# Decay rows of a chunked SSD: stored to memory once and read back by broadcast transfers, in place of 128 selection products on TensorE

## The chip, the cores and the metric

The kernel runs on one core of one Trainium2 chip. The metric is device microseconds of one execution of the whole program; the kernel before takes 1842.9 us, the median of 3 runs (1841.74 to 1843.09). A difference under 0.2% (3.7 us) is about what a measurement of this kernel cannot tell from no change.

## The reference, cut to what matters

One decoder layer on a sequence of 1024 tokens and 1024 channels: an SSD (Mamba-2) mixer and a differential-attention mixer side by side, merged by gates, then a gated conv-FFN. The change lies in the SSD, which works in chunks of 128 tokens, 16 heads in 2 groups of 8. Of one chunk and one head:

```python
a_cum = jnp.cumsum(la, axis=2)
seg = a_cum[:, :, :, None] - a_cum[:, :, None, :]
decay = jnp.exp(jnp.where(causal, seg, -jnp.inf))
cb = jnp.einsum('bclgn,bcsgn->bclsg', cc, bc)
y_diag = jnp.einsum('bclsgr,bcsgrp->bclgrp', cb[..., None] * decay, xd)
```

So for every chunk and head a 128x128 matrix exp(a_cum[l] - a_cum[s]) is wanted, for s up to l, with the running sum of one token set against that of another.

## The kernel before, in words

**Layout.** The kernel holds tokens or channels on the 128 partitions. Wide products are done as three products of float32r halves (high x high, high x low, low x high). `SL` is a ring of 43 slots of 128x1024 float32 in SBUF that tiles take and give back. SyncE (SP) issues nearly all transfers, in the order of the program; a transfer that has to wait holds up all those behind it. At most eight transfers are outstanding, since each waits for the one eight places ahead. PE, DVE, ACT and SP run in an order written out by hand (`tc.manual_schedule`); the order of GpSimd (POOL) and of what lies between those blocks is decided when the program is built.

**Ahead of the SSD.** While the z projection runs (`thirds`, 24 groups of 24 products), `decays_a` and `decays_b` compute dt, the running sum `acum` (128 tokens on the partitions; 8 chunks x 16 heads along the row) and its exponentials. `decays_b` also splits `acum` into a float32r high part and a rest, side by side in `acx` (L866 to L869). `decays_c` (L871 to L877) clears `acT`, turns `acx` chunk by chunk with 8 transposes, and copies the turned rows: `acT` then holds, for each token along the row, the 16 high parts and the 16 rests on 32 partitions.

**The SSD loop.** There are 16 units `u`, one for each chunk and group (`c, g = divmod(u, 2)`). Step `u` of the loop prepares unit `u + 1` and finishes unit `u`. In program order a step does the following.

- `chunk_in(u + 1)`: 4 transposes of x, the product of B and C, a transpose of B, into the PSUM tile `px`; ACT copies them out (L1077, L1078), DVE makes `cbm` and `xd` (L1079, L1080), POOL makes `xdd` and the skip term of `y` (L1082, L1083).
- `chunk_decay(u + 1)`: 8 selection products (L1092), one for each head. The weights are a column of `sel` widened to 128, so that each product adds the head's high part and rest and puts the row a_cum[l] on all 128 partitions of the PSUM tile `pb`. ACT then makes relu(acum[s] - pb) out of PSUM into the decay tile `M[g]` (L1096, 8 instructions) and exp of its negative in place (L1098, 2 instructions).
- `chunk_mask(u + 1, 0)`, and later `(u + 1, 1)`: DVE multiplies half of the decay tile by `cbm` (L1103).
- `chunk_out(u)`: the product with the carried state (`po`, L1110), 8 products with the decay tile as weights (`py`, L1114, each in two passes of 64 columns), and sums on DVE and POOL (L1111, L1116, L1119, L1120).
- `chunk_state(u)`: the product for the next state (`pst`, L1128), and after every second unit `chunk_norm`.

Between these, `fill` puts in products of the v projection (L1028 to L1030, 128x512), `sum_dn` puts in sums of weights for a later stage (L790 to L797 on DVE, with loads `wdr` and stores `wtd`), and `run_bg` puts in small pieces. `M` are two tiles, one for each group. `px` and `pb` take turns in two PSUM buffers (`ps_mm`). SP issues in each step stores of v (`vd`), loads and stores of the weight sums (`wdr`, `wtd`), and by turns the loads of x (`xch`) and z (`zt`) and the store of y (`yd`).

Of the kernel before, what the change touches and what calls it, by code (L numbers as in the profile page):

```python
# [62 lines left out]
def kernel(ctx: ExitStack, tc: tile.TileContext, a: dict, out: bass.AP, dbg=None):  # L63
    nc = tc.nc
    V, A, G, T, SP = nc.vector, nc.scalar, nc.gpsimd, nc.tensor, nc.sync
# [15 lines left out]
    def ps_mm(name):  # L81
        return pmm.tile([P, 2, HALF], F32, tag="mm", name=name, bufs=2)

    def ps_wa(name):
        return pp.tile([P, HALF], F32, tag="wa", name=name, bufs=2)
# [44 lines left out]
    ident = const("ident", [P, P])  # L130
# [279 lines left out]
    SP.dma_start(tri, a["tri"])  # L410
    maskneg = const("maskneg", [P, P])
    SP.dma_start(maskneg, a["maskneg"])
    selr = const("selr", [P, NH])
    SP.dma_start(selr, a["sel"])
    sel = const("sel_r", [P, NH], F32R)

    zd = [dp.tile([P, D], F32, tag=f"zd{i}", name=f"zd{i}") for i in range(8)]
    vd = [dp.tile([P, D], F32, tag=f"vd{i}", name=f"vd{i}") for i in range(8)]
# [180 lines left out]
    part = lambda t, k: t[k // 2][:, k % 2, :]  # L599

    with tc.manual_schedule(engines={EN.PE, EN.DVE, EN.Activation, EN.SP}):
        V.tensor_copy(sel, selr)
        vev = SL.get("vev", F32, (P, 2, HALF))
        cgv = [None, [SL.get(f"xc{n}1") for n in "gv"]]
        for n in ("t2", "t1", "t3"):
# [200 lines left out]

    sm1 = SL.get("sm1", F32, (P, 8, 8, NH))
    sm2 = SL.get("sm2", F32, (P, 1024))
    hi_t = SL.get("hi_t", F32R, (P, 8, NH))
    dtr, dt, la, acum, ea, cd, dte, sp0_ = (sm1[:, n] for n in range(8))  # L810
    acx = sm2[:, 0:256].rearrange("p (c h) -> p c h", c=8)
    sp1_ = sm2[:, 256:384]
    cbm = sm2[:, 384:640].rearrange("p (g l) -> p g l", g=2)
    btok = sm2[:, 640:896].rearrange("p (g l) -> p g l", g=2)
    ev = [SL.get(f"ev{i}", F32, (P, 2, HALF)) for i in range(2)]
    n_ev = 0

    acT = SL.get("acT", F32R, (P, S))
    aexp = const("aexp", [P, NH])

    CH = 8 * NH
    f = lambda t: t.rearrange("p c h -> p (c h)")
# [34 lines left out]
    def decays_b():  # L857
        pa = ps_wa("acum_ps")
        T.matmul(pa[:, :CH], tri, f(la), start=True, stop=True)
        T.matmul(pa[:, CH : 2 * CH], ones, f(la), start=True, stop=True)  # L860
        V.tensor_copy(f(acum), pa[:, :CH])
        A.activation(f(ea), f(acum), AF.Exp)
        A.activation(f(cd), pa[:, CH : 2 * CH], AF.Exp)
        V.tensor_tensor(f(dte), pa[:, CH : 2 * CH], f(acum), op=ALU.subtract)
        A.activation(f(dte), f(dte), AF.Exp)
        hi_r = hi_t  # L866
        V.tensor_copy(hi_r, acum)
        V.tensor_copy(acx[:, :, :NH], hi_r.bitcast(F32))
        V.tensor_tensor(acx[:, :, NH:], acum, hi_r.bitcast(F32), op=ALU.subtract)  # L869

    def decays_c():  # L871
        V.memset(acT.bitcast(F32), 0.0)
        for half in range(2):
            pt = ps_wa(f"acT_ps{half}")
            for q in range(4):
                T.transpose(pt[:32, q * P : (q + 1) * P], acx[:, 4 * half + q, :], ident)
            V.tensor_copy(acT[:32, half * HALF : (half + 1) * HALF], pt[:32, :])  # L877

    dec = None
    adas = [SL.get(f"adas{i}") for i in range(4)]  # L880
# [18 lines left out]
    with tc.manual_schedule(engines={EN.PE, EN.DVE, EN.Activation, EN.SP}):  # L899
        for t_, (c0, wdt) in enumerate(thirds):  # L900
# [4 lines left out]
            for i in range(8):  # L905
                nz = 8 * t_ + i
                ps = (ps_x((1, 3, 2, 0)[nz % 4], f"z{c0}_{i}") if nz < 22 else ps_wa(f"z{c0}_{i}"))[:, :wdt]
                half, q = divmod(i, 4)
# [39 lines left out]
                if nz == 17:  # L948
                    xch = [SL.get(f"xch{i}", F32, (P, KD, P)) for i in range(2)]
# [7 lines left out]
    BT, CT = [xbcT[8], xbcT[9]], [xbcT[10], xbcT[11]]  # L957
    vev = SL.get("vev", F32, (P, 2, HALF))

    SL.put(hi_t)  # L960


    GW = HALF
# [2 lines left out]
    xd = SL.get("xd")  # L966
    xdd = SL.get("xdd")
    xtk = SL.get("xtk")
    M = [SL.get(f"M{g}", F32, (P, RH, P)) for g in range(2)]
    prev = [SL.get(f"prev{i}", F32, (P, 2, GW)) for i in range(2)]  # L970
    tt = SL.get("tt")
    zt = SL.get("zt")
# [89 lines left out]
    def load_z(c):  # L1062
        SP.dma_start(zt, zd[c])
# [21 lines left out]

    def chunk_decay(u):
        c, g, tok, hs, gs, y = at_(u)
        pm = ps_mm(f"pb{c}_{g}")
        for b4 in range(2):
            for r in range(4):  # L1090
                h = g * RH + 4 * b4 + r
                T.matmul(pm[:, b4, r * P : (r + 1) * P], sel[:, h : h + 1].broadcast_to([P, P]), acT[:, tok], start=True, stop=True)  # L1092
        for b4 in range(2):
            for r in range(4):
                h = g * RH + 4 * b4 + r
                A.activation(M[g][:, 4 * b4 + r, :], pm[:, b4, r * P : (r + 1) * P], AF.Relu, scale=-1.0, bias=acum[:, c, h : h + 1])  # L1096
            mv = M[g][:, 4 * b4 : 4 * b4 + 4, :]
            A.activation(mv, mv, AF.Exp, scale=-1.0)  # L1098

    def chunk_mask(u, b4):  # L1100
        c, g, tok, hs, gs, y = at_(u)
        mv = M[g][:, 4 * b4 : 4 * b4 + 4, :]
        V.tensor_tensor(mv, mv, cbm[:, g : g + 1, :].broadcast_to([P, 4, P]), op=ALU.mult)  # L1103

    def chunk_out(u, mask):
        c, g, tok, hs, gs, y = at_(u)
        po = prev[(c + 1) % 2]
        if c > 0:
            pq = ps_wc(f"po{c}_{g}")
            T.matmul(pq, CT[g][:, tok], po[:, g, :], start=True, stop=True)  # L1110
            V.tensor_tensor(v3(tt[:, gs]), v3(pq), bc64(ea[:, c, hs]), op=ALU.mult)  # L1111
        py = ps_wb(f"py{c}_{g}")
        for r in range(RH):
            T.matmul(py[:, r * 64 : (r + 1) * 64], M[g][:, r, :], xd[:, g * GW + r * 64 : g * GW + (r + 1) * 64], start=True, stop=True)  # L1114
        mask()
        V.tensor_tensor(y[:, gs], py, y[:, gs], op=ALU.add)  # L1116
        if c > 0:
            if c < 7:
                G.tensor_tensor(v3(prev[c % 2][:, g, :]), v3(po[:, g, :]), bc64(cd[:, c, hs]), op=ALU.mult)  # L1119
            G.tensor_tensor(y[:, gs], y[:, gs], tt[:, gs], op=ALU.add)  # L1120
# [48 lines left out]
    def fetch_seq(n):  # L1169
        if n < len(seq):  # L1170
            kind, b = seq[n]
            seq_w[n] = wp.tile([P, KD, P], F32, tag="wraw", name=f"{kind}{b}_raw", bufs=3)
            SP.dma_start(seq_w[n].rearrange("p k c -> p (k c)"), a[kind][b])

    load_z(0)
    wdr = [[SL.get(f"wdr{i}{j}", F32, (P, 2, HALF)) for j in range(2)] for i in range(2)]
    wds = [SL.get(f"wds{i}", F32, (P, 2, HALF)) for i in range(2)]
# [8 lines left out]
    with tc.manual_schedule(engines={EN.PE, EN.DVE, EN.Activation, EN.SP}):  # L1186
        for k in range(2):
            down_load(k)
        chunk_in(0)
        fill(2)  # L1190
        chunk_decay(0)
        chunk_mask(0, 0)
        chunk_mask(0, 1)
        lamt = const("lamt", [P, 2, 64])
        lams = const("lams", [P, 2])
        nlam = const("nlam", [P, 1])
        rl = rows[:, R_LAM : R_LAM + 256].rearrange("p (a b d) -> p a b d", a=2, b=2)
        V.tensor_tensor(lamt, rl[:, :, 0, :], rl[:, :, 1, :], op=ALU.mult)
        V.reduce_sum(lams, lamt, axis=AX.X)
        A.activation(lams, lams, AF.Exp)  # L1200
        V.tensor_tensor(nlam, lams[:, 1:2], lams[:, 0:1], op=ALU.subtract)
        V.tensor_scalar(nlam, nlam, -LAM_INIT, None, op0=ALU.add)
        subw = const("subw", [P, 1])
        V.tensor_scalar(subw, vec[:, V_SUB : V_SUB + 1], 1.0 - LAM_INIT, None, op0=ALU.mult)
        fill(4)
        for u in range(16):
            nxt = u + 1 < 16
            if nxt:
                chunk_in(u + 1)
            fill(2)  # L1210
            run_bg(2)
            sum_dn(u, 0)
            if nxt:
                chunk_decay(u + 1)
            run_bg(1)
            sum_dn(u, 1)
            if nxt:
                chunk_mask(u + 1, 0)
            fill(2)
            chunk_out(u, (lambda: chunk_mask(u + 1, 1)) if nxt else (lambda: None))  # L1220
            fill(3)
            run_bg(3)
            sum_dn(u, 2)
            chunk_state(u)
            fill(1 if u % 3 else 0)
            run_bg(1)
            sum_dn(u, 3)
            if u % 2 == 1:
                chunk_norm(u // 2)
            if u == 11:  # L1230
                assert next(sums_dn, None) is None
                SL.put(*wdr[0], *wdr[1], *wds)
                yr = [SL.get(f"yr{i}") for i in range(4)]
                ropc, rops = SL.get("ropc"), SL.get("rops")
                SP.dma_start(ropc, a["ropc"])
                SP.dma_start(rops, a["rops"])
                fetch_seq(0)
                fetch_seq(1)
            elif u == 12:
                load_y(0)  # L1240
        fill(16 * KD)
        run_bg(len(bg))
    SL.put(*yt, xd, xdd, xtk, *M, *prev, tt, zt, acT, sm1, sm2, *xch, *BT, *CT)

# [1113 lines left out]
def host_arrays(i):  # L2358
# [41 lines left out]
        "ident": np.eye(128, dtype=np.float32),  # L2400
        "tri": (s[:, None] <= s[None, :]).astype(np.float32),
        "maskneg": np.where(s[None, :] <= s[:, None], np.float32(0), np.float32(NEG)).astype(np.float32),
        "sel": ((np.arange(128)[:, None] % 16 == np.arange(16)[None, :]) & (np.arange(128)[:, None] < 32)).astype(np.float32),
        "ropc": ropc,
        "rops": rops,
    }
# [14 lines left out]
```

## Time and profile before

| | |
|---|---|
| median of 3 runs | 1842.9 us (1841.74 to 1843.09) |
| span of the profiled execution | 5463.1 us; no time of that execution beside the span is given |
| busy in that span | PE 5447.4, DVE 1312.2, ACT 898.9, POOL 139.0 us |
| moved by transfers | 326.22 MB, mean 60 GB/s over the span |
| SSD loop in that span | from about 1140 to 1740 us |

The profiled execution lasted three times as long as the timed ones. In it the products of TensorE follow one another without a pause, and each takes much longer than a third of the timed run would allow, though the granted clock is shown as full; the other engines are busy for a quarter of the span or less. So its durations on DVE, ACT, POOL and the transfers can be read as they stand, while those on PE have to be scaled, and a wait for PE is longer in it than in a timed run. A row of the views reads: line, engine, operation, tiles out<-in, shapes, count, then busy microseconds and mean nanoseconds of one, then idle time of the engine just before, with what ended it. The chain of waits lists start, length and line of the work that ended last.

### The profile page before, as it was taken

Reading aid. Unit: us, or ns where it says so; the run is one execution under the profiler, and the core shown is the slowest. Engines: PE = TensorE matmul, PEld = TensorE weight load, DVE = VectorE, ACT = ScalarE, POOL = GpSimd, SP = SyncE. Lnnn points to the kernel's source line nnn. Section 1 sums busy time; section 2 is a strip of 40 time slices with the busy share of each in tenths; the row PEclk is TensorE's granted clock in tenths of the full one; section 3 lists DMA queues with packets and bytes.
Section 4 is the critical chain, followed back from the end, with each engine's and each line's share of the span. In section 5 each row is a group of like instructions: output and inputs, shape, how many; then the busy total and the mean of one; then the engine's idle time right before and its main releaser. Section 6 shows DMA issues by size and latency. Waiting matters only on the chain.

```text
span 5463.1 us, 24362 instructions
## 1 busy us (share of the span) xinstructions
PE 5447.4 (100%) x8922; PEld 3303.6 (60%) x8922; DVE 1312.2 (24%) x1984; ACT 898.9 (16%) x1744; POOL 139.0 (3%) x128
## 2 busy tenths in 40 slices
PE   9999999999999999999999999999999999999999
PEld 4555557766665555566677776556555555555555
DVE  4122222222221200022222231212333333332211
ACT  3111110011111100011122221102212111121210
POOL 0000000001110000000000000000000000000000
DMA  4021012212111212121122112210011111123221
GB/s 165 31 77 46 29 35 72 70 64 100 64 67 46 54 35 81 35 52 47 48 72 69 56 47 95 81 46 31 31 44 39 44 35 41 40 71 116 87 63 60
DMA packets 131368, 326.22 MB, mean 60 GB/s; under 512 B 14881, under 2 KB 39089, under 8 KB 131250
## 3 DMA queue, kind: packets, MB, share of 16 engines
q1 hardware_dynamic: 130290, 321.53, 18.2%
q0 software_dynamic: 960, 3.15, 0.2%
q8 instruction: 70, 1.15, 0.1%
q14 instruction: 48, 0.39, 0.0%
HBM read 229.45 MB, written 95.17 MB: 59 GB/s over the span
## 4 chain that ended last, share of the span: by engine, by line
PE 100%; issue 0%; ACT 0%; POOL 0%; DVE 0%; DMA 0%; DVEq 0%; POOLq 0%; ACTq 0%
PE upx L1822 4%; PE upx L1823 4%; PE upx L1821 4%; PE o L1515 4%; PE v L1028 2%; PE z L116 2%; PE v L1029 2%; PE z L118 2%; PE z L117 2%; PE xx L534 2%; PE so L117 2%; PE so L118 2%; PE xx L532 2%; PE upy L1821 2%; PE upy L1822 2%; PE upy L1823 2%
## 5 line engine op out<-in xcount | busy, mean ns | idle before, releaser
L1515 PEld LDWEIGHTS o<-vt,aT 128*128 128x128 f32 x576 | 201.1, 415 | 39.5 <-issue 33.8
L1821 PE MATMUL upx<-t,wu_t 128*128 128x512 f32 x264 | 218.9, 829 | 0.0
L1823 PE MATMUL upx<-t,wu_t 128*128 128x512 f32 x264 | 218.7, 828 | 0.0
L1822 PE MATMUL upx<-t,wu_t 128*128 128x512 f32 x264 | 218.7, 828 | 0.0
L1515 PE MATMUL o<-vt,aT 128*128 128x128 f32 x576 | 214.2, 578 | 0.0
L1456 PE MATMUL sc<-kst,qst 128*128 128x512 f32 (+2 forms) x192 | 141.7, 742 | 0.0
L1457 PE MATMUL sc<-klo,qst 128*128 128x512 f32 (+2 forms) x192 | 141.4, 746 | 0.0
L118 PE MATMUL so<-yT,w_ssd_o_lo 128*128 128x512 f32 x128 | 140.8, 1100 | 0.0
L117 PE MATMUL so<-yT,w_ssd_o_hi 128*128 128x512 f32 x128 | 140.8, 1100 | 0.0
L116 PE MATMUL so<-yT,w_ssd_o_hi 128*128 128x512 f32 x128 | 139.3, 1088 | 0.0
L1503 ACT COPY aT<-at 128x512 f32<-128x512 f32 (+2 forms) x96 | 45.9, 479 | 562.2 <-PE at L1502 562.2
L1822 PEld LDWEIGHTS upx<-t,wu_t 128*128 128x128 f32 x264 | 93.5, 354 | 63.8 <-issue 63.8
L1821 PEld LDWEIGHTS upx<-t,wu_t 128*128 128x128 f32 x264 | 93.4, 354 | 63.7 <-issue 62.7
L1823 PEld LDWEIGHTS upx<-t,wu_t 128*128 128x128 f32 x264 | 92.3, 350 | 63.8 <-issue 63.8
L1114 PEld LDWEIGHTS py<-xd,M 128*128 128x128 f32 x256 | 107.1, 596 | 34.8 <-issue 34.8
L1028 PE MATMUL v<-wv_hi,hT 128*128 128x512 f32 x96 | 121.5, 1266 | 0.0
L116 PE MATMUL z<-wz_hi,hT 128*128 128x346 f32 (+1 forms) x144 | 121.1, 841 | 0.0
L118 PE MATMUL z<-wz_hi,hT 128*128 128x346 f32 (+1 forms) x144 | 119.7, 832 | 0.0
L117 PE MATMUL z<-wz_lo,hT 128*128 128x346 f32 (+1 forms) x144 | 119.1, 827 | 0.0
L1502 PE MATMUL at<-ident,p 128*128 128x128 f32 x288 | 117.1, 576 | 0.0
L2184 PE MATMUL dx<-wdt_hi,g_hi 128*128 128x512 f32 x132 | 109.5, 830 | 0.0
L2186 PE MATMUL dx<-wdt_hi,g_lo 128*128 128x512 f32 x132 | 109.2, 827 | 0.0
(553 smaller groups left out, 10212.8 us busy)
## 6 DMA issues: line engine op xcount, KB each, us to landing
adas<-in_w_ada SPq DMA_DIRECT2D x32, 512.0 KB, 3.9
wdr<-in_w_down SPq DMA_DIRECT2D x22, 512.0 KB, 5.5
wtd<-wds SPq DMA_DIRECT2D x22, 512.0 KB, 2.9
wuf<-in_w_up SPq DMA_DIRECT2D x22, 512.0 KB, 3.5
gld_s<-gsum SPq DMA_DIRECT2D x22, 512.0 KB, 2.6
gst<-gld_s SPq DMA_DIRECT2D x20, 512.0 KB, 4.3
wdt_raw<-wtd SPq DMA_DIRECT2D x20, 512.0 KB, 3.9
wuv<-in_w_up SPq DMA_DIRECT2D x19, 512.0 KB, 3.6
```

What stands on the lines that cost most here:

```text
L116: T.matmul(ps, lh, rh, start=(i == 0), stop=False)
L117: T.matmul(ps, lh, rl, start=False, stop=False)
L118: T.matmul(ps, ll, rh, start=False, stop=(i == n - 1))
L1028: T.matmul(ps, xh_, wh, start=(k == 0), stop=False)
L1456: T.matmul(sc[:, n0:n1], qs_[s][:, tsl], ks_[s][:, n0:n1], start=True, stop=False)
L1457: T.matmul(sc[:, n0:n1], qs_[s][:, tsl], kl[s][:, n0:n1], start=False, stop=True)
L1502: T.transpose(ptr[:, k * P : (k + 1) * P], pt_[i % 2][0][:, (k0 + k) * P : (k0 + k + 1) * P], ident)
L1515: T.matmul(po_of[j, grp][:, qi, :], at[:, k, :], vt[j % 2][:, kt, :], start=(kt == 0), stop=(kt == i))
L1821: T.matmul(out_, wh, xh_, start=(k == 0 and first), stop=False, skip_group_check=not first)
L1822: T.matmul(out_, wh, xl_, start=False, stop=False, skip_group_check=not first)
L1823: T.matmul(out_, wl, xh_, start=False, stop=(k == end), skip_group_check=not first)
L2184: T.matmul(o, gh[:, kk, tsl], wh, start=(k == 0 and not more), stop=False, skip_group_check=more)
```

## The change

The 128 selection products, the split of `acum`, `acT`, `sel` and its load go. `decays_c` now turns `acum` once (128 tokens x 128 chunk-head pairs), copies the result out of PSUM and stores it to memory as `acd`, 16 rows of 1024, one for each unit: 8 heads x 128 tokens. `load_decay(u)` reads row `u` into a decay tile with the row repeated on all 128 partitions (a transfer of 512 KB on the SP queue). ACT's relu then works in place in that tile, reading SBUF where it read PSUM. There are three decay tiles in place of two, used in turn. The first three are loaded ahead of the loop; the load for unit `u + 2` stands at the start of step `u`, from step 1 on, ahead of `chunk_in(u + 1)`; its tile is that of unit `u - 1`, so that it waits for the products `py` of that unit. In the built program POOL also does the skip term (L1083) in another place among its instructions, and a subtraction (L637) that stood behind the copy of `sel` on DVE at the start of the program stands earlier.

```diff
-    selr = const("selr", [P, NH])
-    SP.dma_start(selr, a["sel"])
-    sel = const("sel_r", [P, NH], F32R)
...
-        V.tensor_copy(sel, selr)
...
-    hi_t = SL.get("hi_t", F32R, (P, 8, NH))
-    acx = sm2[:, 0:256].rearrange("p (c h) -> p c h", c=8)
+    acr = sm2[:, 0:128]
-    acT = SL.get("acT", F32R, (P, S))
+    acd = dp.tile([2 * 8, D], F32, tag="acd", name="acd")
...
-        hi_r = hi_t
-        V.tensor_copy(hi_r, acum)
-        V.tensor_copy(acx[:, :, :NH], hi_r.bitcast(F32))
-        V.tensor_tensor(acx[:, :, NH:], acum, hi_r.bitcast(F32), op=ALU.subtract)
...
     def decays_c():
-        V.memset(acT.bitcast(F32), 0.0)
-        for half in range(2):
-            pt = ps_wa(f"acT_ps{half}")
-            for q in range(4):
-                T.transpose(pt[:32, q * P : (q + 1) * P], acx[:, 4 * half + q, :], ident)
-            V.tensor_copy(acT[:32, half * HALF : (half + 1) * HALF], pt[:32, :])
+        pt = ps_wa("acT_ps")
+        T.transpose(pt[:, :P], f(acum), ident)
+        V.tensor_copy(acr, pt[:, :P])
+        SP.dma_start(acd.rearrange("u (r t) -> (u r) t", t=P), acr)
...
-    M = [SL.get(f"M{g}", F32, (P, RH, P)) for g in range(2)]
+    Ms = [SL.get(f"M{i}", F32, (P, NH // 2, P)) for i in range(3)]
+
+    def load_decay(u):
+        if u < 16:
+            SP.dma_start(Ms[u % 3].rearrange("p r t -> p (r t)"), acd[u : u + 1, :].broadcast_to([P, D]))
...
     def chunk_decay(u):
         c, g, tok, hs, gs, y = at_(u)
-        pm = ps_mm(f"pb{c}_{g}")
         for b4 in range(2):
             for r in range(4):
                 h = g * RH + 4 * b4 + r
-                T.matmul(pm[:, b4, r * P : (r + 1) * P], sel[:, h : h + 1].broadcast_to([P, P]), acT[:, tok], start=True, stop=True)
-        for b4 in range(2):
-            for r in range(4):
-                h = g * RH + 4 * b4 + r
-                A.activation(M[g][:, 4 * b4 + r, :], pm[:, b4, r * P : (r + 1) * P], AF.Relu, scale=-1.0, bias=acum[:, c, h : h + 1])
-            mv = M[g][:, 4 * b4 : 4 * b4 + 4, :]
+                m_ = Ms[u % 3][:, 4 * b4 + r, :]
+                A.activation(m_, m_, AF.Relu, scale=-1.0, bias=acum[:, c, h : h + 1])
+            mv = Ms[u % 3][:, 4 * b4 : 4 * b4 + 4, :]
             A.activation(mv, mv, AF.Exp, scale=-1.0)
...
+    for u in range(3):
+        load_decay(u)
     load_z(0)
...
         for u in range(16):
             nxt = u + 1 < 16
+            if u > 0:
+                load_decay(u + 2)
             if nxt:
                 chunk_in(u + 1)
```

`chunk_mask` and `chunk_out` read `Ms[u % 3]` where they read `M[g]`.

More of the change, by code (lines that the diff above doesn't have):

```diff
@@ L958 @@
     vev = SL.get("vev", F32, (P, 2, HALF))
-    SL.put(hi_t)
     GW = HALF
@@ L1101, in chunk_mask @@
         c, g, tok, hs, gs, y = at_(u)
-        mv = M[g][:, 4 * b4 : 4 * b4 + 4, :]
+        mv = Ms[u % 3][:, 4 * b4 : 4 * b4 + 4, :]
         V.tensor_tensor(mv, mv, cbm[:, g : g + 1, :].broadcast_to([P, 4, P]), op=ALU.mult)
@@ L1113, in chunk_out @@
         for r in range(RH):
-            T.matmul(py[:, r * 64 : (r + 1) * 64], M[g][:, r, :], xd[:, g * GW + r * 64 : g * GW + (r + 1) * 64], start=True, stop=True)
+            T.matmul(py[:, r * 64 : (r + 1) * 64], Ms[u % 3][:, r, :], xd[:, g * GW + r * 64 : g * GW + (r + 1) * 64], start=True, stop=True)
         mask()
@@ L1242 @@
         run_bg(len(bg))
-    SL.put(*yt, xd, xdd, xtk, *M, *prev, tt, zt, acT, sm1, sm2, *xch, *BT, *CT)
+    SL.put(*yt, xd, xdd, xtk, *Ms, *prev, tt, zt, sm1, sm2, *xch, *BT, *CT)
     def load_qk(m, q_, khi_, klo_):
@@ L2402, in host_arrays @@
         "maskneg": np.where(s[None, :] <= s[:, None], np.float32(0), np.float32(NEG)).astype(np.float32),
-        "sel": ((np.arange(128)[:, None] % 16 == np.arange(16)[None, :]) & (np.arange(128)[:, None] < 32)).astype(np.float32),
         "ropc": ropc,
```

## Prediction

> **What bounds the kernel now.** I read the page's first lines, then the chain of waits, then the windows. The page says that TensorE is never free, and that the chain that ended last runs on it alone.
>
> ```profile
> span 5463.1 us, 24362 instructions
> PE 5447.4 (100%) x8922; PEld 3303.6 (60%) x8922; DVE 1312.2 (24%) x1984; ACT 898.9 (16%) x1744; POOL 139.0 (3%) x128
> ...
> PE 100%; issue 0%; ACT 0%; POOL 0%; DVE 0%; DMA 0%; DVEq 0%; POOLq 0%; ACTq 0%
> ```
>
> But this span is three times the timed 1842.9 us, so PE's pace has to be read before anything is taken from it. In the windows below (length, then busy time and count of PE, PEld, DVE, ACT, POOL; clock; share of the 16 DMA engines; GB/s), 300 to 600 and 4000 to 4600 us hold nothing but products of 512 columns; the chain shows where the pace changes.
>
> ```profile
> 300.00:600.00 300.00, 300.00 (x367) 156.78 (x366) 68.25 (x100) 38.21 (x60) 0.00 (x0) 1.00 0.17 53
> 1140.00:1740.00 600.00, 600.00 (x932) 375.41 (x931) 134.25 (x195) 92.98 (x247) 83.32 (x63) 1.00 0.20 72
> 4000.00:4600.00 600.00, 600.00 (x1009) 354.72 (x1008) 201.50 (x258) 115.25 (x171) 0.00 (x0) 1.00 0.11 40
> ```
>
> ```profile
> 2680.46 0.84 PE gap L1411
> 2681.30 0.62 PE gap L1412
> ```
>
> ```profile
> 0.00:85.00 85.00, 75.22 (x88) 35.13 (x89) 57.96 (x107) 47.58 (x88) 3.98 (x8) 1.00 0.70 266
> ```
>
> One 512-column product takes 300/367 = 0.817 us until about 2682 us, and 600/1009 = 0.595 us after. So PE was held back in the profiled execution, by a different amount in its two parts, though the clock column says 1.00. The timed pace follows from the total: the first 85 us hold 58 us of DVE work, which is not slowed, so I leave them about 60 us. The remaining 1783 us cover (2682 - 85)/0.817 = 3179 products' worth and (5463 - 2682)/0.595 = 4674, so one product takes at most 1783/7853 = 0.227 us, and a PE time of the first part shrinks by 0.227/0.817 = **0.278** at most. What lies around the span is not shown; it sits inside these 1783 us, which is why the factor is an upper end. The SSD loop (1140 to 1740 us) is then at most 167 us of a timed run. Its other engines do not shrink: DVE has 134 us of work in it, ACT 93, POOL 83, and the DMA engines 0.20 x 600 = 120. So in a timed run PE bounds this loop by a fifth, not by four times as the page suggests.
>
> **The change, part by part. PE.** One step of the loop in the chain:
>
> ```profile
> 1382.07 1.52 PE px L1072 x4
> ...
> 1389.06 0.68 PE v L1030
> 1389.74 2.79 PE pb L1092 x8
> 1392.53 1.02 PE v L1028
> 1393.55 0.84 PE v L1029
> ...
> 1397.75 3.20 PE po L1110 x2
> 1400.95 6.16 PE py L1114 x16
> ...
> 1418.08 1.68 PE px L1072 x4
> ```
>
> The 8 selection products take 2.79 us, and the product behind them 1.02 in place of 0.84. Sixteen times 2.97 is 47.5 us of the profiled span; times 0.278 that is 13.2 us. That is the upper end. The lower end counts columns alone: 128 products of 128 columns are 32 products of 512, so 7.3 us. I take 12, near the row of the operation itself: `py` with 64 columns costs 6.16/16 = 0.385 us, more than the 0.35 of these with 128, so it is not columns that pace small products here. The Trainium skill's page "TensorE: Matmul & The Clock Gate", section "Back-to-back issue gap", gives about 81 ns for a product of 128 columns in a stream with its weight load; by that the sum would be 10.4 us, inside the same bounds, and no run here shows that figure.
>
> In the z stage 8 transposes become one.
>
> ```profile
> 1056.97 3.20 PE acT_ps L876 x8
> ```
>
> ```profile
> L877 DVE CAST acT<-acT_ps 32x512 fp32r<-32x512 f32 x2 | 1.4, 679 | 0.4 <-PE acT_ps L876 0.3
> L872 DVE MEMSET acT<- 128x1024 f32 x1 | 0.9, 912 | 0.2 <-issue 0.2
> L861 DVE COPY sm<-acum_ps 128x128 f32<-128x128 f32 x1 | 0.3, 292 | 0.5 <-PE acum_ps L860 0.5
> ```
>
> That is 7/8 of 3.20 us, 0.8 us after scaling. DVE loses the clearing, two copies and the split (L867 to L869) for one copy like L861, some 2.7 us, worth nothing: PE is the later engine there. **Total off PE: 12.8 us** (8 to 14).
>
> **ACT.** Its instructions stay, 8 relus and 2 exps in each step, but the relu reads SBUF. The nearest rows are four activations of 128x128 from SBUF at the start, and the four relus from PSUM:
>
> ```profile
> 18.94 1.27 ACT L212 ACTIVATE hr<-ident,rs 128x128 f32<-128x128 f32 x4
> ```
>
> ```profile
> 1354.05 1.14 ACT L1096 ACTIVATE M<-pb,sm 128x128 f32<-128x128 f32 x4 [6.87 <-PE pb L1092]
> ```
>
> So about 0.03 us more each, 4 us in all, on an engine with 93 of 167 us used: nothing. A wait goes as well:
>
> ```profile
> ACT M L1096 <- PE pb L1092: 102.5, 16, 7.1
> ```
>
> ACT need no longer wait for the selection products; it can begin when `px` is copied out, if the tile has landed. That lengthens DVE's room for the mask, and by itself moves no end.
>
> **The transfers.** Sixteen loads of 512 KB come in, 8.4 MB. Thirteen of them are issued in steps 1 to 13. Their price on the DMA engines comes from the windows of the loop:
>
> ```profile
> 1140.00:1250.00 110.00, 110.00 (x179) 70.82 (x177) 28.04 (x42) 22.37 (x61) 12.35 (x10) 1.00 0.21 69
> 1250.00:1350.00 100.00, 100.00 (x154) 62.06 (x155) 25.90 (x38) 11.41 (x32) 17.25 (x13) 1.00 0.24 87
> 1350.00:1450.00 100.00, 100.00 (x158) 63.36 (x157) 22.54 (x32) 18.80 (x45) 14.74 (x10) 1.00 0.24 87
> 1450.00:1550.00 100.00, 100.00 (x151) 60.25 (x150) 23.54 (x32) 16.17 (x46) 17.98 (x13) 1.00 0.20 69
> 1550.00:1650.00 100.00, 100.00 (x157) 62.39 (x156) 20.71 (x33) 12.10 (x33) 14.48 (x11) 1.00 0.25 91
> 1650.00:1740.00 90.00, 90.00 (x139) 56.54 (x139) 13.52 (x20) 12.12 (x30) 6.52 (x6) 1.00 0.07 25
> ```
>
> In 1250 to 1350 us the engines are busy 24 us for 8.7 MB, so 512 KB cost 1.45 us. Now compare the three loads window by window, after the change. PE has 4, 2, 3, 3, 2 and 2 groups of selection products fewer; scaled it needs 27.3, 26.1, 25.3, 25.3, 26.1 and 23.4 us. DVE needs 28.0, 25.9, 22.5, 23.5, 20.7 and 13.5. The DMA engines, with 2, 3, 2, 3, 3 and 0 loads more, need 26.0, 28.4, 26.9, 24.4, 29.4 and 6.3. So PE is passed by DVE in the first window by 0.7 us, and by the transfers in the second, third and fifth by 2.3, 1.6 and 3.3: 7.9 us in all, if nothing spreads from window to window. The transfers do spread, since loads run one to two steps ahead of their use and stores are waited for a step later. I take half, **4 us given back**; both ends (0 and 7.9) go into the range. Whether a load that repeats one row runs at the same price is not shown by a row of its own; a halved rate would add 13 x 1.45 = 19 us to the engines, and that end is in the slower rival.
>
> The page "DMA: Bandwidth & Descriptors" of the Trainium skill, section "Where 436 GB/s comes from", sets the ceiling at 435 GB/s; by it the second window's 8.7 + 1.6 MB take 23.7 us, less than PE's 26.1, and nothing would be given back. The trace's own share (24 us for 8.7 MB, 363 GB/s) lies under that ceiling, so it speaks for the dearer price.
>
> **When a load arrives.** The first three stand late in the z stage on SP. Tiles 0 and 1 are issued ahead of the last four groups of z, each about 24 x 0.56 us x 0.278 = 3.7 us long, so some 15 us ahead of the loop. In the loop the load for unit u + 2 stands first in step u and is wanted by ACT early in step u + 1: a step (36 to 38 us of the span, 10 us scaled, 9.3 after) and the 2 us until `px` is copied out, 11 us. The nearest load, and what SP waits for in this stretch:
>
> ```profile
> zt<-zd SPq DMA_DIRECT2D x8, 512.0 KB, 3.6
> ```
>
> ```profile
> SPq L1044 <- ACT vev L1043: 186.6, 12, 31.0
> SPq L793 <- DVE wds L792: 123.6, 8, 22.5
> ```
>
> Landing takes 3.6 us when the queue is short. The load stands behind the last store of weight sums of step u - 1, so it is issued when DVE has done that sum, perhaps 2 to 4 us into step u. That leaves 3 to 5 us. Its own wait (for `py` of unit u - 1, done a third of a step before) adds nothing, and what is queued behind it (`xch`, `zt`, `vd`) waits for later work. If a load is late, ACT stands still, and behind it the copies of v and of the next `px`; PE feels it only when `py` of that unit is due, half a step later. So I cost the wait at nothing; without that cover it costs what the slower rival says. The moved L637 and the dropped copy of `sel` at the start, and the slots that later tiles get, I cost at 0, between -1 and +1 us; POOL's moved skip term is wanted only by the sum behind `py`, so nothing too.
>
> **Sum.** 1842.9 - 12.8 + 4 = **1834 us**. The terms off PE are 47.5 and 2.8 us of the profiled span; the sum is carried to the median through the factor 0.278, not through the span itself. A profile with PE as slow as this one would show the whole 50 us gone.
>
> **The rivals.**
> - *The transfers have room*, as the cited ceiling has it, and PE bounds the whole loop: 12.8 to 14 us come through, **1830**. For it: the average over the loop, 120 + 23 = 143 us of DMA work for 154 of PE. Against it: three windows.
> - *DVE takes over, and the gain is hidden.* DVE and POOL get in each other's way:
>
> ```profile
> L1103 DVE TENSOR_TENSOR M<-M,sm 128x512 f32<-128x512 f32 x32 | 22.0, 688 | 91.1 <-ACT M L1098 91.1
> L1080 DVE TENSOR_TENSOR xd<-xtk,sm 128x512 f32<-128x512 f32 x16 | 16.7, 1041 | 0.0
> ```
>
> The same operation takes 0.69 us, but 1.04 on average where POOL's L1083 runs beside it. In a timed run POOL's 83 us lie in 154 us and not in 600, so more of its 63 instructions meet DVE at work. If another 30 of them cost DVE 0.7 us (a bit over the difference, which is an average), DVE has 155 us, as much as PE after the change; with waits it is the later one, and all but 0 to 3 us are hidden: **1841**. The Trainium skill's page "SBUF — State Buffer", section "Who interferes with whom", has the rule: a DVE instruction with two SBUF inputs and a GpSimd instruction that reads SBUF block each other. The trace agrees with 1041 against 688 ns.
> - *The loads come late, and the loop goes by the transfers.* If the DMA queue is full, a load waits behind eight others (8 x 1.45 = 11.6 us) and behind SP's own wait. From 11 us between its place and its landing on, ACT stands; from about 16 us on, PE does. Then ten steps take the transfers' 28.4 / 2.7 = 10.5 us and about 1 us of SP's wait, 11.5 in place of 10.2, and the other six save 0.8 each: 13 - 5 = +8, **1851**. At half rate for repeated rows it would be more, about 1860.
> - *That the products don't go* is out: the built program has none of the 128 left.
>
> **How the numbers follow.** Forecast (1830 to 1839, a part given back) 0.40; transfers have room (under 1830) 0.14; hidden (within 0.2% of before, 1839.2 to 1846.6) 0.24; late loads (over 1846.6) 0.22. So faster by over 0.2% 0.54, within 0.2% (about what a measurement of this kernel can tell from no change) 0.24, slower 0.22. The forecast's own range is 1830 to 1839. For 8 in 10 I go down to 1827 (the 14 us and 2 us for the unknown clock) and up to 1851, leaving the worst of the late loads out.
>
> **What would show it.** Right: no `pb` in the chain, the loop shorter by 48 us in a profile with PE as slow as here, `M` waiting for its transfer for less than a few us, the new loads landing in 3 to 8 us. Wrong: L1085 (the relu) of ACT waiting for the load in most steps, with `py` of PE behind it (late loads); or a shorter profile but unchanged times (DVE). If a profile at full PE pace shows DVE busy through the loop, the second rival is the cause. The step that I trust least is the share of the transfers that spreads.

## The result, and the profile after

The kernel after takes **1840.1 us** (median of 20 executions, 1837.6 to 1843.4), the kernel before in the same job 1843.0 (20 executions, 1841.7 to 1844.2). The ratio is 0.9985, 95% interval 0.9979 to 0.9991: 2.8 us faster, where 9 us were forecast. That lies in the band of the second rival (the gain is hidden, 1839.2 to 1846.6, named price 1841), not in the forecast's.

The profiled execution of after ran at full pace: 1841.7 us timed, span 1839.9. That of before, on which the prediction rests, did not, so the two cannot be set side by side. The kernel before was therefore profiled again (run `before_full` below: 1843.1 us timed, span 1840.9). All comparisons here are with that profile. First lines of the page of after, and of `before_full`:

```profile
span 1839.9 us, 24115 instructions
PE 1805.2 (98%) x8787; PEld 1507.6 (82%) x8787; DVE 1295.0 (70%) x1978; ACT 896.3 (49%) x1744; POOL 143.6 (8%) x128
```

```profile
span 1840.9 us, 24362 instructions
PE 1817.4 (99%) x8922; PEld 1521.4 (83%) x8922; DVE 1299.6 (71%) x1984; ACT 893.1 (49%) x1744; POOL 140.7 (8%) x128
```

PE has 12.2 us less to do; the span is 1.0 us shorter. So about 11 us of PE time turned into idle time. The SSD loop tells where. The windows view over it (length; busy and count of PE, PEld, DVE, ACT, POOL; clock; DMA share; GB/s), first `before_full`, then after; the last row of each is the whole stretch:

```profile
335.00:377.00 42.00, 42.00 (x243) 35.05 (x241) 38.79 (x58) 26.43 (x74) 18.11 (x14) 1.00 0.66 226
377.00:419.00 42.00, 42.00 (x237) 34.04 (x236) 37.46 (x52) 23.61 (x65) 24.90 (x18) 1.00 0.90 334
419.00:461.00 42.00, 41.29 (x226) 32.93 (x226) 38.16 (x50) 22.16 (x58) 25.32 (x18) 1.00 0.70 240
461.00:503.00 42.00, 42.00 (x235) 34.17 (x234) 28.03 (x41) 21.41 (x56) 16.18 (x13) 1.00 0.65 234
...
335.00:503.00 168.00, 167.29 (x935) 136.19 (x934) 142.44 (x197) 93.61 (x250) 84.51 (x62) 1.00 0.73 258
```

```profile
335.00:377.00 42.00, 38.44 (x192) 30.96 (x191) 34.16 (x55) 26.39 (x72) 18.13 (x14) 0.92 0.75 265
377.00:419.00 42.00, 40.22 (x211) 31.10 (x210) 38.00 (x51) 24.13 (x65) 24.87 (x18) 1.00 1.00 365
419.00:461.00 42.00, 37.10 (x190) 28.49 (x190) 37.74 (x48) 22.31 (x59) 26.14 (x18) 1.00 0.82 292
461.00:503.00 42.00, 42.00 (x223) 33.50 (x222) 30.56 (x45) 22.82 (x57) 18.28 (x15) 1.00 0.77 283
...
335.00:503.00 168.00, 157.76 (x810) 124.06 (x809) 140.45 (x196) 95.65 (x249) 87.42 (x63) 0.98 0.83 301
```

Before, PE is idle for 168 - 167.3 = 0.7 us of the stretch; after, for 10.2. All of it lies in the first three rows, where VectorE (DVE) is busy 114.4 of 126 us before and 109.9 after; in the last row, where the sums of down weights end (at 469.7 us in after) and DVE has room, PE is full in both. How long the loop is comes from the first and last start of `px` and `py` (min/median/max ns, then first and last start), `before_full` first:

```profile
L1072 PE MATMUL px<-ident,xch x64: 270/272/274, 335.8 to 488.0; 128*128 128x128 f32 x64
...
L1114 PE MATMUL py<-xd,M x256: 218/275/275, 346.1 to 502.7; 128*128 128x64 f32 x128
```

```profile
L1065 PE MATMUL px<-ident,xch x64: 270/273/421, 335.0 to 487.2; 128*128 128x128 f32 x64
...
L1103 PE MATMUL py<-xd,M x256: 217/275/275, 343.4 to 500.9; 128*128 128x64 f32 x128
```

With 0.3 us for the last product, 167.2 us before and 166.2 after. After's also starts 0.8 us earlier, as much as was worked out for the 7 transposes of the z stage. Whom PE waited for in the loop of after, in us, times and longest (the same view of `before_full` has one row, 0.7 us for `wv_lo`):

```profile
PE pst L1117 <- DVE tt L1100: 8.3, 5, 3.6
PE v L1021 <- ACT wv_hi L1008: 1.2, 1, 1.2
PE v L1022 <- DVE wv_lo L1009: 0.8, 1, 0.8
```

`pst` (the product for the next state) and `po` share one PSUM bank (`ps_wc`, one buffer). `pst` may begin when DVE has read `po` into `tt`, and `tt` stands in DVE's list behind the sums and half a mask. One of these waits in the timelines of DVE and of PE:

```profile
362.32 0.69 DVE L786 TENSOR_TENSOR wds<-wdr 128x512 f32<-128x512 f32 x1 [3.33 <-DMA wtd<-wds]
363.04 0.69 DVE L788 TENSOR_TENSOR wds<-wdr,wds 128x512 f32<-128x512 f32 x1
...
365.59 1.53 DVE L791 TENSOR_TENSOR wds<-wdr,wdr 128x512 f32<-128x512 f32 x1
367.04 0.68 DVE L793 TENSOR_TENSOR wds<-wdr,wds 128x512 f32<-128x512 f32 x1
367.64 0.68 DVE L1092 TENSOR_TENSOR M<-M,sm 128x512 f32<-128x512 f32 x1
368.25 0.68 DVE L1100 TENSOR_TENSOR tt<-po,sm 128x512 f32<-128x512 f32 x1
```

```profile
365.12 0.39 PE L1023 MATMUL v<-wv_hi,hT 128*128 128x512 f32 x1
369.07 2.04 PE L1117 MATMUL pst<-xdd,sm 128*128 128x512 f32 x2 [3.56 <-DVE tt L1100]
370.12 1.42 PE L1021 MATMUL v<-wv_hi,hT 128*128 128x512 f32 x1
371.34 0.63 PE L1022 MATMUL v<-wv_lo,hT 128*128 128x512 f32 x1
```

DVE stood 3.3 us for a store of sums, then worked off its list without a pause and reached `tt` at 368.3; PE stood from 365.5 to 369.1. The same step of `before_full`:

```profile
367.64 0.68 DVE L1111 TENSOR_TENSOR tt<-po,sm 128x512 f32<-128x512 f32 x1
369.83 1.02 PE L1128 MATMUL pst<-xdd,sm 128*128 128x512 f32 x2
```

With the selection products on PE, DVE reached this `tt` at 367.6 us, no later than in after (there it stood 0.6 us for the store and not 3.3, but a sum took 1.49 us against 0.69 and `xd` 1.26 against 0.68). PE came to `pst` 1.5 us after `tt` had ended and did not wait. In `one_load`, without the loads, `tt` starts at 367.8. So taking the products off PE let PE arrive earlier, but not DVE. In after, PE came back slowly: the products behind the gap take 1.42 and 0.63 us where 0.39 is usual. The next two rows show why:

```profile
369.00:375.00 6.00, 5.93 (x16) 4.24 (x17) 5.02 (x10) 1.02 (x4) 3.87 (x3) 0.50 0.96 350
375.00:381.00 6.00, 6.00 (x34) 4.92 (x33) 5.67 (x9) 3.81 (x11) 1.68 (x2) 1.00 1.03 414
```

For 6 us after the gap the granted clock is 0.50 and PE is busy throughout: by an estimate from that row, 3 us more are lost. Last, the new loads, and ACT's wait for them:

```profile
M<-acd SPq DMA_DIRECT2D x16, 512.0 KB, 6.6
```

```profile
ACT M L1085 <- DMA M<-acd: 6.1, 3, 2.1
```

They land in 6.6 us (median) and keep ACT waiting three times, 6.1 us in all. PE's products never wait for `M`; of its weight loads for `py`, the view puts waits of 0.2 us at a time, 1.7 us in all, down to that relu.

### The profile page after: what moved, and what is told of

Read it like the earlier page. It is cut to its first block, busy times and chain, and to the rows that moved or that the text cites. A ratio compares the mean times of both kernels' runs of the same rounds, so it can differ in the third digit from the quotient of the medians.

```text
span 1839.9 us, 24115 instructions
## 1 busy us (share of the span) xinstructions
PE 1805.2 (98%) x8787; PEld 1507.6 (82%) x8787; DVE 1295.0 (70%) x1978; ACT 896.3 (49%) x1744; POOL 143.6 (8%) x128
## 4 chain that ended last, share of the span: by engine, by line
PE 65%; DVE 5%; ACT 3%; issue 1%; DMA 1%; POOL 0%; DVEq 0%; POOLq 0%; ACTq 0%
PE upx L1815 4%; PE upx L1816 4%; PE upx L1814 4%; PE o L1508 3%; PE upy L1815 2%; PE upy L1814 2%; PE upy L1816 2%; PE dx L2178 2%; PE dx L2179 2%; PE dx L2177 2%; PE at L1495 2%; PE dy L2178 2%; PE dy L2179 2%; PE dy L2177 2%; PE sc L1450 2%; PE ao L118 2%
## 5 line engine op out<-in xcount | busy, mean ns | idle before, releaser
L1814 PE MATMUL upx<-t,wu_t 128*128 128x512 f32 x264 | 103.2, 391 | 0.5 <-DVE cv L2242 0.4
L1815 PE MATMUL upx<-t,wu_t 128*128 128x512 f32 x264 | 102.8, 390 | 0.2 <-DVE t L1932 0.2
L1816 PE MATMUL upx<-t,wu_t 128*128 128x512 f32 x264 | 102.7, 389 | 0.0
L1508 PEld LDWEIGHTS o<-vt,aT 128*128 128x128 f32 x576 | 75.3, 191 | 9.2 <-ACT aT L1496 4.6
L1508 PE MATMUL o<-vt,aT 128*128 128x128 f32 x576 | 80.8, 276 | 0.4 <-ACT aT L1496 0.2
L1469 DVE TENSOR_REDUCE nmx<-sc 128x1 f32<-128x640 f32 (+3 forms) x64 | 65.6, 1025 | 2.2
L1449 PE MATMUL sc<-kst,qst 128*128 128x512 f32 (+2 forms) x192 | 63.7, 340 | 0.0
L1450 PE MATMUL sc<-klo,qst 128*128 128x512 f32 (+2 forms) x192 | 63.2, 346 | 0.0
L1832 DVE SCALAR_TENSOR_TENSOR ug<-cg,vec,ug 128x1023 f32<-128x1023 f32 (+1 forms) x44 | 56.3, 1280 | 6.1 <-ACT ug L1831 5.3
L1814 PEld LDWEIGHTS upx<-t,wu_t 128*128 128x128 f32 x264 | 49.5, 188 | 11.7 <-DVE cv L2242 1.3
L1815 PEld LDWEIGHTS upx<-t,wu_t 128*128 128x128 f32 x264 | 49.6, 188 | 10.7 <-DVE t L1932 0.5
L1816 PEld LDWEIGHTS upx<-t,wu_t 128*128 128x128 f32 x264 | 49.6, 188 | 10.3
L1832 DVE SCALAR_TENSOR_TENSOR uv<-cv,vec,uv 128x1023 f32<-128x1023 f32 (+1 forms) x44 | 56.2, 1278 | 0.9 <-ACT uv L1831 0.9
L2177 PE MATMUL dx<-wdt_hi,g_hi 128*128 128x512 f32 x132 | 51.3, 389 | 0.0
```

The lines of the kernel that those rows point to most:

```text
L1449: T.matmul(sc[:, n0:n1], qs_[s][:, tsl], ks_[s][:, n0:n1], start=True, stop=False)
L1450: T.matmul(sc[:, n0:n1], qs_[s][:, tsl], kl[s][:, n0:n1], start=False, stop=True)
L1469: V.reduce_max(nmx[:, bq, s : s + 1], sc[:, :L], axis=AX.X, negate=True)
L1508: T.matmul(po_of[j, grp][:, qi, :], at[:, k, :], vt[j % 2][:, kt, :], start=(kt == 0), stop=(kt == i))
L1814: T.matmul(out_, wh, xh_, start=(k == 0 and first), stop=False, skip_group_check=not first)
L1815: T.matmul(out_, wh, xl_, start=False, stop=False, skip_group_check=not first)
```

## The experiments

Each is compared with the kernel before, run on the same chip in the same job; times are medians. After's own ratio is 0.9985 (0.9979 to 0.9991). What an edit gives over after is the difference of two such ratios, and nearly all of the intervals overlap after's a little, so these gains are uncertain by 1 to 1.5 us, that of `half_sums` by 2 (estimates from the spread of the executions). What a kernel leaves out is said in its expectation. "DVE takes over" is the theory that the loop now waits for DVE's list; "the forecast" is that PE still paces it and transfers give some back; the third theory is that the loads cost what the products did.

**The kernel before at full pace** (`before_full`, no edit).

> The kernel before, as it is, for a profile at full PE pace. The forecast (TensorE sets the loop's length, its 128 products are worth 12 us) expects the loop, from the first px transposes to the last py, to be some 9 to 12 us longer than the 166 us of the kernel after, with TensorE busy nearly all of it and hardly a wait of it on VectorE. The rival that VectorE takes over expects about 169 us here too, so that the products lie in time in which TensorE would wait for VectorE otherwise. A third theory, that the loads cost what the products did, expects the forecast's length here, a DMA share well under that of after's loop (0.77 to 0.98 in its stretches) and no long waits of TensorE.

1843.1 us. The loop is 167.2 us, 1.0 longer than after's and not 9 to 12; of the three, the second rival's 169 with little change between the kernels is nearest. PE is idle 0.7 us, DVE busy 142 of 168. In the profiled executions, then, the change moves the loop by less than a tenth of what it takes off PE.

**The products alone** (`few_products`).

```diff
+                if b4 == r == 0:
-                T.matmul(pm[:, b4, r * P : (r + 1) * P], ...
+                    T.matmul(pm[:, b4, r * P : (r + 1) * P], ...
...
-                A.activation(M[g][:, 4 * b4 + r, :], pm[:, b4, r * P : (r + 1) * P], AF.Relu, ...
+                A.activation(M[g][:, 4 * b4 + r, :], pm[:, 0, :P], AF.Relu, ...
```

> The kernel before with one selection product in each step in place of eight; every relu reads that one's result, so the decay tiles are wrong, and nothing is loaded for them. It is the taking away alone. The forecast: 112 of 128 products gone, 7/8 of 12 us, so 10 to 11 us under the kernel before, 1832. VectorE takes over: 2 to 4 us under before, 1839 to 1841, with TensorE waiting for VectorE in the loop. The loads cost what the products did: as the forecast here, 1832.

1838.7 us, ratio 0.9979 (0.9970 to 0.9988): 4.0 us. Without any load and with 112 products gone, only 4 of the 11 us come through. The middle of its loop, and its PE waits:

```profile
377.00:461.00 84.00, 78.69 (x409) 60.83 (x408) 80.94 (x103) 46.16 (x123) 54.30 (x36) 1.00 0.80 285
```

```profile
PE pst L1129 <- DVE tt L1112: 7.0, 5, 1.7
```

DVE is busy 80.9 of 84 us there. The gain is lost with no load in play, so the loads are not the main cause.

**The change without its loads** (`one_load`).

```diff
     def load_decay(u):
-        if u < 16:
+        if u == 2:
...
-                m_ = Ms[u % 3][:, 4 * b4 + r, :]
-                A.activation(m_, m_, AF.Relu, ...
+                A.activation(Ms[u % 2][:, 4 * b4 + r, :], Ms[2][:, 4 * b4 + r, :], AF.Relu, ...
```

> The kernel after with one of its 16 decay loads; every step's relu reads that one tile and writes one of two others, so the decay tiles are wrong. It is the change without its transfers. The forecast put their price at 4 us: 1836. VectorE takes over: within 1 us of after, 1839 to 1841. The loads cost what the products did: 8 to 9 us under after, 1831 to 1832.

1838.4 us, ratio 0.9976 (0.9968 to 0.9985), so 4.3 us under before and some 1.5 under after, between the 1836 of the forecast and the 1839 of DVE. In its profile the loop is 162.1 us (`px` from 335.3, `py` to 497.5), of which PE is idle 9.0:

```profile
PE pst L1116 <- DVE tt L1099: 8.9, 5, 2.8
```

PE's own time in the loop is thus 153.1 us, against 166.5 before: **the products were worth 13.4 us of PE**. They are gone, and 8.3 us of new idle time has come in their place. In after PE's own time is 155.9 with the same products; the 2.8 us between agree with the 3 us of the stretch at half clock. The third theory, which expected 1831 to 1832, is refuted: the loads cost about 1.5 us in the median.

**Less work on DVE, in after and in before** (`half_sums`, `half_sums_before`; the same edit).

```diff
-        V.tensor_tensor(t2, b22, t1, op=ALU.subtract)
+        if k == 0:
+            V.tensor_tensor(t2, b22, t1, op=ALU.subtract)
...
-        V.tensor_tensor(t4, b21, t2, op=ALU.subtract)
+        if k == 0:
+            V.tensor_tensor(t4, b21, t2, op=ALU.subtract)
```

> The kernel after with two of the four block differences of the down weights (t2 and t4, about 1.0 and 1.27 us each on VectorE in the loop) made for the first block alone, so 20 VectorE operations, some 22 us of work, fewer in the loop and the down product's weights wrong; transfers as in after. VectorE takes over: 5 to 9 us under after, 1831 to 1835, and the wait of pst on tt goes. The forecast, and the theory of the loads: within 2 us of after.

> The kernel before with the same 20 block differences (t2 and t4, all but the first block's) left out, so the down product's weights are wrong. The theory that VectorE takes over only once the products are gone: before is held by TensorE alone (0.7 us idle in its 167.2 us of loop), so within 1 us of the kernel before, 1842 to 1843, against 4 us that the same edit gave the kernel after. A rival, that less VectorE work helps any kernel by as much (fewer collisions with GpSimd, earlier transfers): 1838 to 1839.

In after: 1835.9 us (six executions, 1833.4 to 1841.0), ratio 0.9969 (0.9957 to 0.9982), 3 to 4 us under after, short of the 5 to 9 expected. In before: 1842.3 us, ratio 0.9998 (0.9989 to 1.0007), nothing. That pair is the strongest evidence: the same DVE work costs nothing that can be told with the products there, and some 3 to 4 us without them. The wait of `pst` on `tt` was expected to go and only fell, in a profiled execution of 1833.4 us, the shortest of the six:

```profile
PE pst L1119 <- DVE tt L1102: 3.7, 2, 2.1
```

**Less work on GpSimd, in after and in before** (`no_skip`, `no_skip_before`).

```diff
+        if c < 2:
-        G.tensor_tensor(v3(y[:, gs]), v3(xtk[:, gs]), ...
+            G.tensor_tensor(v3(y[:, gs]), v3(xtk[:, gs]), ...
```

> The kernel after with GpSimd's skip term (16 operations) made for the first two chunks alone, so y is wrong from the third on; 12 GpSimd operations fewer in the loop, VectorE's list as in after. If VectorE is stretched by GpSimd (the mask's mean is 852 ns, 680 undisturbed) and this is what makes its chain late: mask mean 780 ns or less and 2 to 4 us under after, 1836 to 1838. If GpSimd's share in it is small: within 1 us of after.

> The kernel before with no_skip's edit, 12 GpSimd operations fewer in the loop, so y is wrong from the third chunk on. VectorE's chain is late only where the products are gone: within 1 us of before, 1842 to 1843.5, against the 2.6 us that the edit gave the kernel after. If GpSimd's operations hold any kernel: 1840 to 1841.

In after 1837.6 us, ratio 0.9972 (0.9962 to 0.9983), 2.5 under after; in before 1842.4, ratio 0.9999 (0.9990 to 1.0008). DVE's operations with two inputs in SBUF are stretched where GpSimd works beside them. The mask over the loop, in `before_full`, in after and in `no_skip` (count, then busy us and mean ns):

```profile
L1103 DVE TENSOR_TENSOR M<-M,sm 128x512 f32<-128x512 f32 x32 | 24.2, 762 | 5.6 <-ACT M L1098 5.5
```

```profile
L1092 DVE TENSOR_TENSOR M<-M,sm 128x512 f32<-128x512 f32 x32 | 26.5, 831 | 6.3 <-ACT M L1087 6.3
```

```profile
L1093 DVE TENSOR_TENSOR M<-M,sm 128x512 f32<-128x512 f32 x32 | 24.3, 761 | 6.8 <-ACT M L1088 6.8
```

762 ns, 831 and 761, against 680 undisturbed. So a part of DVE's lateness is GpSimd's, as the second rival had it.

**Another bank for `pst`** (`pst_slot`), **the scaling of y on ACT** (`y_scale_act`), **both** (`pst_and_scale`).

```diff
-        pst = ps_wc(f"pst{c}_{g}")
+        pst = ps_mm(f"pst{c}_{g}")[:, 0, :]
```

```diff
-                V.tensor_scalar(y[:, gs], y[:, gs], ssy[:, c, g : g + 1], 0.5, op0=ALU.mult, op1=ALU.mult)
+                A.activation(y[:, gs], y[:, gs], AF.Copy, scale=ssy[:, c, g : g + 1])
...
-            lambda: rstd_of(ssy[:, c, :], ssy[:, c, :], 1.0 / (4 * GW), 1e-5),
+            lambda: rstd_of(ssy[:, c, :], ssy[:, c, :], 1.0 / GW, 4e-5),
```

> The kernel after with the state product's PSUM tile in the pair of banks that the selection products used before, no longer in the one bank that it shares with po; nothing else differs. If the stall is that shared bank (pst waits until VectorE has read po, 8.3 us in 5 waits), TensorE runs on: 1834 to 1837. If VectorE's throughput is the bound, the wait moves to the next thing that it must make (prev, xd, the mask's second half) and little is won: 1838 to 1840. The forecast's theory, that the transfers take what is missing: within 1 us of after.

> The kernel after with the norm's scaling of y (14 to 16 VectorE operations of 0.76 us, 10.1 us in the loop) on ScalarE, the half folded into the mean's scale; the same result. If VectorE's throughput is the bound: half of what 22 us fewer gave, 2 us under after, 1838. If only the shared bank stalls TensorE: 1839 to 1840.

> The two edits pst_slot and y_scale_act together in the kernel after. If VectorE's time and the shared bank both hold TensorE, their gains add: 1832 to 1835. If one hides the other: the better of the two alone. What is left above 1830 would be the transfers.

`pst_slot`: 1837.4 us, ratio 0.9972 (0.9962 to 0.9983), 2.5 under after, each against the kernel before of its own job. That lies just over the 1834 to 1837 expected of the shared bank. The wait of `pst` is gone; what PE waits for now:

```profile
PE v L1022 <- DVE wv_lo L1009: 4.5, 2, 3.6
PE po L1099 <- DVE tt L1100: 1.3, 1, 1.3
```

The edit also let 16 products of the q projection start ahead of the loop's end, so it is not the bank alone. `y_scale_act` **missed**: 1842.3 us, ratio 0.9995 (0.9986 to 1.0004), 2 us over after, though DVE's time in the loop fell from 140.5 to 130.0 us. Its waits:

```profile
ACT yt L1136 <- POOL ssy L139: 28.0, 6, 6.1
DVE sm L1072 <- ACT sm L1071: 16.2, 9, 2.8
```

ACT works in order too. Scaling y, it stood 28 us for GpSimd's root, and the copies of the next unit behind it came late, for which DVE then stood 16 us. So what counts is not DVE's busy time but when DVE gets to `tt`. Both together: 1838.3 us, ratio 0.9978 (0.9969 to 0.9986), no better than the bank alone.

**Earlier loads for v** (`v_early`; `pst_v` with the other bank; `pst_v_one_load` with one decay load as well).

```diff
-                if vh == 0 and i == 5:
+                if vh == 0 and i == 3:
```

> The kernel after with the three loads of the v weights' second half issued two token blocks earlier (at the fourth of eight in place of the sixth); nothing else differs. In after ScalarE waited 7.0 us for the first of them and TensorE 1.9 us in two waits behind it. If that late load is a price of its own: 1 to 2 us under after, 1838 to 1839. If VectorE's chain is the only thing that holds: within 0.7 us of after.

> The kernel after with both pst_slot and v_early. In pst_slot TensorE's one long wait, 4.5 us in two, was for the low part of the v weights, behind a load that came 6.8 us late. If the transfers now set that wait: 3 to 4 us under pst_slot, 1833 to 1835. If VectorE's time is what is left: the wait moves on, within 1 us of pst_slot, 1836 to 1838.

> pst_v with one of the 16 decay loads, as in one_load (decay tiles wrong). It shows what the products' place on TensorE is worth when neither the shared bank nor the late load of v holds it: by the forecast's 12.8 us and what else the loop keeps, 1830 to 1832. Against pst_v it prices the loads: 1 to 3 us if they cost as little as one_load showed, 4 or more if the transfers are what pst_v still waits for.

`v_early`: 1839.7 us, ratio 0.9984 (0.9975 to 0.9993), nothing that can be told from after. `pst_v`: 1837.0 us, ratio 0.9968 (0.9956 to 0.9980), hardly better than `pst_slot`. The expectations took the wrong load: the late one is the fourth, which stays where it was (issued at 420 us in after and in `pst_v`), since its buffer, one of three, comes free only then; a fourth buffer was not tried. `pst_v_one_load`: 1835.8 us, ratio 0.9962 (0.9950 to 0.9975), again short of the 1830 to 1832 expected, with 5.2 us of PE idle left in its loop. The loads are worth 1.2 us here.

**The order in DVE's list** (`tt_first`; `pst_tt` with the other bank).

```diff
-            if nxt:
-                chunk_mask(u + 1, 0)
             fill(2)
-            chunk_out(u, (lambda: chunk_mask(u + 1, 1)) if nxt else (lambda: None))
+            chunk_out(u, (lambda: [chunk_mask(u + 1, 0), chunk_mask(u + 1, 1)]) if nxt else (lambda: None))
```

> The kernel after with VectorE's list of a step reordered by one operation: tt, which empties the bank that pst waits for, ahead of the first half of the next step's mask instead of behind it; the same operations on every engine, the same result. If pst's stall is the order in VectorE's list (the mask, 0.85 us and a wait for ScalarE of 6.3 us in all, stands ahead of tt): 1 to 3 us under after, 1837 to 1839, with less of the wait of pst on tt. If VectorE is simply full: within 1 us of after, the wait at another place.

> pst_slot with tt_first's order as well. With the bank no longer shared by po and pst, tt's place matters only to the next po: within 1 us of pst_slot, 1836.5 to 1838.5. If the order of VectorE's list holds TensorE by another way too: under 1836.

`tt_first`: 1839.4 us, ratio 0.9984 (0.9975 to 0.9993) against after's 0.9985, so nothing that can be told, though in its profiled execution (1836.8 us, its shortest) the wait of `pst` on `tt` is 4.3 us. `pst_tt`: 1837.1 us, ratio 0.9971 (0.9958 to 0.9983), as `pst_slot`. One place earlier in the list is worth less than the list's length.

**A version that beats both** is `pst_v`, 1837.0 us, 6.0 under before and 3.1 under after; `pst_slot` with its single line is as good within the intervals.

## Why the prediction was wrong

**PE's pace and the loop's length: right.** At most 167 us were worked out for the loop from the slowed profile; it is 167.2 at full pace. The loop also starts 0.8 us earlier, as was worked out for the z stage; no run isolates that.

**The products on PE: right, a little low.** 12 us were taken, 13.2 was the upper end; PE's own time in the loop fell by 13.4 in `one_load` and by 11.4 for 112 products in `few_products` (166.5 - 155.1), 0.10 us each.

**ACT and the new wait: right.** The relu takes 388 ns from SBUF against 368 from PSUM in `before_full` (medians), 0.02 us more each, and ACT waits 6.1 us for the loads, with none of PE's products waiting for `M`. The loads land in 5.1 to 11.4 us, not 3 to 8.

**Transfers give 4 us back: the sign right, the size too large.** By the ratios the loads cost 1.5 us; 1.2 in the other pair. The DMA share rose to 1.00 in 377 to 419 us, at 365 GB/s, which is the rate that was taken. So the queues did fill for that stretch, but it cost less than half of what I took.

**The comparison of PE with DVE, window by window, is the step that failed.** It found DVE ahead of PE in one window alone, by 0.7 us, let that stand among the 7.9 us of which half was taken, and put DVE at nothing in the other five. What the runs showed in its place is 8.3 us (`one_load`) to 9.5 us (after) of new idle time of PE; of all its idle time in the loop, 8.9 of 9.0 us and 8.3 of 10.2 are `pst` waiting for DVE's `tt`. Two things were wrong in the step. First, the DVE times came from a profile in which GpSimd's operations lay three times as far apart. At full pace DVE has 142 us in the loop of before where 134 were counted; the first three windows of `before_full` give 114 of 126 us. Secondly, it asked only which engine has more work. DVE needs no 100% to hold PE: it works in order and waits itself, for ACT, GpSimd and transfers, and PE stands whenever DVE's list reaches `tt` later than PE reaches `pst`. The wait views of before, with PE three times as slow, could not show that. I priced this rival by DVE's total (155 us) and gave it 0.24. Its time (1841) came out, partly by luck: DVE's total in after's loop is 140 us, not 155. Its reason holds in part: 12 GpSimd operations are worth 2.5 us (`no_skip`), and 20 of DVE's own 3 to 4 (`half_sums`).

**The account, for the two profiled executions.** PE's own time in the loop -13.4, new idle time +9.5, half clock +2.8: -1.1 us, and the loop is 1.0 shorter. With 0.8 us ahead of it and 0.8 given back behind it, the spans differ by 1.0. The medians differ by 2.8: 4.3 for the change without its loads, whose profiled execution lies at its median, less 1.5 for the loads.

The half clock was no term of the sum, and it shows in the times. Of after's 20 executions the four with a mean granted clock of 0.997 took 1842.2 us on average, those with 0.998 and 0.999 both 1839.9, and the two with 1.000 took 1837.9. The kernel before, at 0.998 to 1.000 wherever its clock is listed, spreads over 2.4 us, after over 5.8. So the ends of after's spread go with the clock. An execution with longer pauses would have both the longer time and the lower clock, so what the clock alone costs was not shown, nor why one execution has more of these stretches than another.

**Open** is how the 5 us of idle time in the best versions would go: the late fourth load of v was not moved, and a version with both fewer sums and the other bank was not run.

## What to carry to other kernels

When work is taken off the engine that paces a stage, look first at the engine that is busy nine tenths of that stage and works in order: the gain is what is left until that engine's next hand-over comes late, and a PSUM bank shared by two products is such a hand-over. Judge it from a profile at the timed pace, since in a slowed one every other engine seems to have room. To find out afterwards, take the same work off the suspected engine in both kernels: it costs nothing in one and shows in the other.

## What the runs showed of the hardware

A pause of PE can cost more than its length. After the 3.56 us gap in after the granted clock was 0.50 for 6 us. In `pst_v` two gaps of 2.15 and 1.43 us, 8.5 us apart, kept it there for the whole of this first row:

```profile
414.00:424.00 10.00, 8.57 (x27) 6.26 (x25) 9.40 (x13) 2.97 (x6) 5.35 (x4) 0.50 0.95 338
424.00:434.00 10.00, 9.24 (x50) 7.29 (x49) 9.22 (x9) 7.01 (x18) 8.56 (x5) 0.99 0.41 145
```

PE is busy for 8.57 of these ten us. Its 512-column products start 0.43 us apart there and 0.23 us apart after it, so about 4 us are lost (an estimate), on top of the 3.6 us of the gaps. It is not a matter of the gap's length alone: a gap of 2.83 us in `one_load` left the clock at 1.00, and after one of 1.26 us in `tt_first` it was 0.53 from 420.0 to 423.5 us. The Trainium skill's page "TensorE: Matmul & The Clock Gate", section "Part 1: The HAM clock gate (the "warmup" mystery)", says that the clock is halved after an idle window of about 3.4 us, in windows that run freely. The halving agrees with the 0.50 here; the two gaps of `pst_v`, each shorter than that window, do not.
